# Eight raw weight tiles and three row tiles in the v half of a PEER layer

## The chip, the core and the metric

The kernel runs on one core of one Trainium2 chip. The metric is the device time of one execution in microseconds; the kernel before takes 3439.81 us, the median of three runs (3434.23 to 3440.13).

## What is computed

One layer of a diffusion backbone over 512 latent tokens of width 2048. The part that matters here is the second half of the layer, a retrieval of single-neuron experts (PEER). For every token 128 of 16384 experts are chosen (8 heads, 16 each), and the output is a weighted sum of their rows:

```python
u = u_tab[expert]
v = v_tab[expert]
act = jax.nn.gelu(jnp.einsum('nd,ned->ne', hb, u), approximate=False) * gate
return jnp.einsum('ne,ned->nd', act, v)
```

`u_tab` and `v_tab` have 16384 rows of 2048 float32 values, 128 MB each. The result, times a gain, is added to the residual stream and is the output.

## The kernel before

Float32 products are made of three passes in a rounded float32 format: each operand is split into `hi` (rounded) and `lo` (the remainder), and `mm3` (L102) issues hi x hi, hi x lo and lo x hi. For weights the split is made on the fly by `weights` (L93): a DMA on SyncE's queue brings a raw tile of 128x1024 float32 (512 KB, `raw_tile`, L88), ScalarE makes `whi` from it (L98), VectorE makes `wlo` (L99). There are four buffers for each of `raw`, `whi` and `wlo`. A raw buffer is free for the next DMA when its `wlo` is made; a `whi` or `wlo` buffer when the matmuls that read it are done.

The layer first computes modulations, projections, attention and convolution, the output projection and the choice of experts. Then come two halves over the expert tables:

- **The u half** (`u_block`, L515, 128 blocks). For 352 of the tokens the products with all 16384 experts are computed densely from streamed tiles of `uT`. The other 160 tokens go another way: `gather` (L715) lets GpSimd fetch one expert row for each of 128 token lanes (`row`, 128x2048, 1 MB, an indirect DMA, L723), 160 times in all, and `use_u` (L736) has VectorE form the dot products. The normalised activations lie in `HH` and `HL`, and in token-major form in `h2row` and `h2ext`.
- **The v half** (loop L846 to L882). The dense part is 16 groups of 8 units. A unit takes two tiles of `vb`, and accumulates two of the 16 output columns `m` in PSUM with 2 x 24 matmuls of 128x352. Every fourth column stays in PSUM over all groups (`held`, `hps` in the trace); the others are added by VectorE into `acc` (L877) after each unit. `Ah` and `Al` of a group are made a group ahead by `prepare` (L775): `load_group` (L767) loads `gt` and `gl` on SyncE's queue, VectorE multiplies (L784), ScalarE and VectorE split (L787, L789). Beside it, `gather` fetches 160 rows of `v`, and `use_v` (L743) has VectorE add each row, times its coefficient in `dots`, into the accumulator `accg` (L745). `gather` keeps two rows in flight: it fetches the next row after each use. `paced` spreads the 160 uses over the first 15 groups. In the last group `finish` (L829) adds everything to the residual and stores it.

Each engine runs its instructions in one fixed order, set when the program is built: a scheduler takes the program's order, gives tiles to buffers, and may move an instruction ahead of others that have to wait for a buffer. On VectorE the row accumulations, the `wlo` tiles, the `acc` additions and the `gl`/`Al` work thus stand in one queue; on SyncE the raw tiles and the `gt`/`gl` loads; on GpSimd the gathers. Memory is given out by pools: `vl` (L823), the v half's own pool, is opened after the u half's pools `us` and `hs` are closed and takes their room, so a tile in it waits until the last reader of what lay there is done. For `HH` and `HL` this is TensorE's last matmul of the u half. The pool `wp` lives through the whole kernel.

Of the kernel before, what the change touches and what calls it, by code (L numbers as in the profile page):

```python
# [10 lines left out]
F32 = mybir.dt.float32  # L11
# [3 lines left out]
AF = mybir.ActivationFunctionType  # L15
ALU = mybir.AluOpType
# [4 lines left out]
P = 128  # L21
T, D, L, KD = 512, 2048, 256, 16
# [5 lines left out]
ND = T - NG  # L28
# [14 lines left out]
def build(nc, tc, ap, es):  # L43
# [3 lines left out]
    wp = es.enter_context(pool("wp"))  # L47
# [38 lines left out]
    RAWB, HB, LB = 4, 4, 4  # L86

    def raw_tile(src, shape):  # L88
        raw = wp.tile(shape, F32, tag="raw", bufs=RAWB, name="raw")
        nc.sync.dma_start(raw, src)  # L90
        return raw

    def weights(src, eng=None):  # L93
        shape = list(src.shape)
        raw = raw_tile(src, shape)
        hi = wp.tile(shape, F32R, tag="whi", bufs=HB, name="whi")
        lo = wp.tile(shape, F32R, tag="wlo", bufs=LB, name="wlo")
        weights.hi = nc.scalar.activation(hi, raw, AF.Copy)  # L98
        weights.lo = (eng or nc.vector).tensor_tensor(lo, raw, hi.bitcast(F32), op=ALU.subtract)  # L99
        return hi, lo  # L100
# [28 lines left out]
    rings = {}  # L129

    def psum(role, name, *shape):
        banks = BANKS[role]
        turn = rings[role] = rings.get(role, -1) + 1
        t = pp.tile([P, 512], F32, tag=f"b{banks[turn % len(banks)]}", name=name)
        if len(shape) == 3:
            return t[:shape[0], 0:shape[1] * shape[2]].rearrange("p (a b) -> p a b", b=shape[2])
        return t[:shape[0], 0:shape[1]]
# [37 lines left out]
    def project(m, ctx):  # L175
        if m not in started:
            project_half(m, ctx, 0)
        project_half(m, ctx, 1)
        return started[m]
# [122 lines left out]
    def run_tasks(gen, n):  # L302
        for _ in range(n):
            if next(gen, 0) == 0:
                return
# [3 lines left out]
    with pool("att", side="right", **reuse) as att:  # L309
# [55 lines left out]
        for hd in range(NH):  # L365
            qps, _ = project(3 * hd, False)
# [23 lines left out]
    with pool("cnv", side="right", **reuse) as cnv:  # L390
# [11 lines left out]
        for g in range(8):  # L402
            cps, _ = project(24 + 3 * g, False)
# [5 lines left out]
            ups, _ = project(25 + 3 * g, False)  # L409
# [11 lines left out]
            bps, _ = project(26 + 3 * g, False)  # L421
# [59 lines left out]
    NS = P + NX  # L481
    h2row = gp.tile([P, KD, P], F32, name="h2row")
    h2ext = gp.tile([P, KD, P], F32, name="h2ext")
    exi = gp.tile([P, NS], I32, name="exi")
    gtg = gp.tile([P, NS], F32, name="gtg")
    dots = gp.tile([P, NS], F32, name="dots")
# [26 lines left out]
    mark = {}  # L513

    def u_block():  # L515
        i = u_block.n
        u_block.n += 1
        ps = psum("u", "sps", P, ND)
        for hf in range(2):
            w = weights(ap["uT"][i, hf])  # L520
            for k in range(8):
                kk = 8 * hf + k
                mm = mm3(ps, (w[0][:, k, :], w[1][:, k, :]), (HH[:, kk, 0:ND], HL[:, kk, 0:ND]), kk == 0, kk == KD - 1)
        mark["pe"], mark["dve"], mark["act"] = mm, weights.lo, weights.hi
        if i % 2 == 0:
            u_block.out = uo.tile([P, 2, ND], F32, tag="ug", bufs=2, name="ug")
        nc.scalar.activation(u_block.out[:, i % 2, :], ps, AF.Gelu)
        if i % 2 == 1:
            nc.scalar.dma_start(gu[i // 2], u_block.out)
# [124 lines left out]
    urow = us.enter_context(pool("urow", **reuse))  # L654
# [57 lines left out]
        if o + 4 == CH:  # L712
            nc.scalar.dma_start(gd[tok // CH], scatter.stg)

    def gather(tab, rp, use):  # L715
        rows = []

        def fetch():
            s = len(rows)
            if s == NS:  # L720
                return
            row = rp.tile([P, KD, P], F32, tag="row", bufs=2, name="row")
            nc.gpsimd.indirect_dma_start(out=row.rearrange("p k d -> p (k d)"), out_offset=None, in_=ap[tab],  # L723
                                         in_offset=bass.IndirectOffsetOnAxis(ap=exi[:, s:s + 1], axis=0))
            rows.append(row)

        fetch()
        fetch()
        yield
        for s in range(NS):  # L730
            with tc.issue_after(mark["dve"].ins):
                use(s, rows[s])
            fetch()
            yield
# [7 lines left out]

    def use_v(s, row):  # L743
        ag = accg[0 if s < P else 1]
        nc.vector.scalar_tensor_tensor(ag, row, dots[:, s:s + 1], ag, op0=ALU.mult, op1=ALU.add)  # L745

    def paced(gen, steps, units):
        state = [0, 0]

        def step():  # L750
            state[0] += 1
            want = min(steps, -(-state[0] * steps // units))
            while state[1] < want:
                state[1] += 1
                run_tasks(gen, 1)

        return step
# [4 lines left out]
    gat_u = None  # L762
# [31 lines left out]
    while u_block.n < 128:  # L794
        u_block()
        n = u_block.n
        if gat_u is None:
            gat_u = paced(gather("u", urow, use_u), NS + 1, 128 - n)
        gat_u()
        for x in built:  # L800
            scatter(*x)
        built = ready
        ready = []
        if hots:
            for _ in range(1):
                x = next(hots, 0)
                if x == 0:
                    hots = None
                    break
                if x:  # L810
                    ready.append(x)
        elif not built and va is None:
            gbs.close()
            pqs.close()
            va = vs.enter_context(pool("va", side="right", **reuse))
        if va and n >= 116:
            first = first or prepare(0, va)
            run_tasks(first, 1)
# [2 lines left out]
    hs.close()  # L821

    vl = vs.enter_context(pool("vl", **reuse))  # L823
    acc = vl.tile([P, KD, ND], F32, name="acc")
    accg = [vl.tile([P, KD, P], F32, name=f"accg{i}") for i in range(2)]
    for x in accg:
        nc.gpsimd.memset(x, 0.0)

    def finish(m):  # L829
        if m % 2 == 0:  # L830
            finish.x = vl.tile([P, 2, T], F32, tag="fin", bufs=2, name="xm")
            nc.sync.dma_start(finish.x, x1d[m:m + 2].rearrange("m p t -> p m t"))
        xm = finish.x[:, m % 2, :]
        g2c = mod2[:, 48 + m:49 + m]
        src = held[m] if m in held else acc[:, m, :]
        nc.vector.scalar_tensor_tensor(xm[:, 0:ND], src, g2c, xm[:, 0:ND], op0=ALU.mult, op1=ALU.add)
        tp = psum("fin", "tp", P, NG)
        nc.tensor.matmul(tp[:, 0:NX], accg[1][:, m, :], selq, start=True, stop=True)
        nc.tensor.transpose(tp[:, NX:NG], accg[0][:, m, :], ident)
        nc.vector.scalar_tensor_tensor(xm[:, ND:T], tp, g2c, xm[:, ND:T], op0=ALU.mult, op1=ALU.add)  # L840
        nc.sync.dma_start(ap["out"][:, m, :], xm)

    NGV = NGRP // 2
    held = {}
    gat_v = paced(gather("v", vl, use_v), NS + 1, 8 * (NGV - 1))
    for g in range(NGV):  # L846
        hi, lo = A[g]
        nxt = None
        if g + 1 < NGV:
            nxt = prepare(g + 1, va if g % 2 else vl)  # L850
        for dq in range(8):
            ws = [weights(ap["vb"][2 * g + q, dq]) for q in range(2)]
            mark["dve"] = weights.lo
            pss = []
            for x in range(2):
                m = 2 * dq + x
                if m % 4 == 3:
                    if g == 0:
                        held[m] = psum("held", "hps", P, ND)
                    pss.append(held[m])  # L860
                else:
                    pss.append(psum("v", "ops", P, ND))
            for q in range(2):
                w = ws[q]
                for x in range(2):
                    for b in range(NB):
                        mm3(pss[x], (w[0][:, b, P * x:P * x + P], w[1][:, b, P * x:P * x + P]),
                            (hi[:, NB * q + b, :], lo[:, NB * q + b, :]), q + b == 0 and (g == 0 or 2 * dq + x not in held),
                            q == 1 and b == NB - 1 and (g == NGV - 1 or 2 * dq + x not in held))
            for x in range(2):  # L870
                m = 2 * dq + x
                if m in held:
                    pass
                elif g == 0:
                    nc.scalar.activation(acc[:, m, :], pss[x], AF.Copy)
                else:
                    mark["dve"] = nc.vector.tensor_tensor(acc[:, m, :], acc[:, m, :], pss[x], op=ALU.add)  # L877
                if g == NGV - 1:
                    finish(m)
            gat_v()  # L880
            if nxt:
                run_tasks(nxt, 1)  # L882
# [69 lines left out]
```

## Time and profile before

| what | value |
|---|---|
| median of three runs | 3439.81 us |
| the profiled execution | 3443.56 us |
| its span, first to last instruction | 3441.8 us |
| TensorE busy (PE) | 3287.1 us, 96% of the span |
| VectorE busy (DVE) | 2492.6 us, 72% |
| ScalarE busy (ACT) | 1177.3 us, 34% |
| GpSimd busy (POOL) | 670.8 us, 19% |
| mean granted TensorE clock | 0.982 of full speed |
| HBM traffic | 909 MB, 264 GB/s over the span |

PE is TensorE, DVE VectorE, ACT ScalarE, POOL GpSimd and SP SyncE; a q behind a name is an engine's issuing part. The tiles carry the program's names. The durations of neighbouring matmuls overlap, so the pace of TensorE is read from how many run in a stretch, not from the duration of one. "DMA share" is the mean busy share of the core's 16 DMA engines.

### The profile page before, as it was taken

The page shows a single profiled execution, that of the slowest core. Times are in us where ns is not written, and L with a number is a line of the kernel's source. Part 1 is how long each engine was busy: PE and PEld are TensorE (multiplying, and loading weights), DVE is VectorE, ACT ScalarE, POOL GpSimd, SP SyncE. Part 2 cuts the span into 40 slices and gives each one's busy share as a digit, 9 for nine tenths or more (in the row PEclk, how much of TensorE's full clock was granted, in tenths as well). Part 3 has the DMA queues.
Part 4 walks back from the last instruction along what each step waited for, and adds up shares of the span by engine and source line. Part 5 has one row for each costly group of instructions (what it writes and reads, how often), then busy time and mean ns, then how long its engine had stood idle before and what let it go on. Part 6 is the DMA issues. An engine that isn't in the chain of part 4 may idle for free.

```text
span 3441.8 us, 48157 instructions
## 1 busy us (share of the span) xinstructions
PE 3287.1 (96%) x18951; PEld 3019.0 (88%) x18951; DVE 2492.6 (72%) x3648; ACT 1177.3 (34%) x1582; POOL 670.8 (19%) x402
## 2 busy tenths in 40 slices
PE   5899999999999988999999999999989989989999
PEld 1488888878887878999999999999989989989999
DVE  4444444888756888787888887676787887878885
ACT  3344444222324454333333333333222222322222
POOL 0000000000001663222211222222323223322320
PEclk9999999999999999999999999999999999999999
DMA  8722222888772226999999999998898998989986
GB/s 303 234 67 63 66 66 61 289 278 286 242 237 85 86 83 229 334 341 336 339 343 337 328 339 340 355 360 303 319 344 316 343 343 322 353 328 336 338 323 210
DMA packets 265316, 912.52 MB, mean 265 GB/s; under 512 B 23809, under 2 KB 77313, under 8 KB 222721
## 3 DMA queue, kind: packets, MB, share of 16 engines
q1 hardware_dynamic: 208208, 527.74, 44.6%
q0 software_dynamic: 46080, 335.56, 25.7%
q10 hardware_dynamic: 10800, 46.14, 3.4%
q8 instruction: 149, 2.44, 0.3%
q14 instruction: 79, 0.64, 0.1%
HBM read 854.82 MB, written 54.53 MB: 264 GB/s over the span
## 4 chain that ended last, share of the span: by engine, by line
PE 63%; DMA 19%; DVE 10%; issue 4%; POOL 2%; ACT 1%; SPq 0%; DVEq 0%; ACTq 0%; POOLq 0%
DMA row<-v,exi 11%; PE sps L105 8%; PE sps L103 8%; PE sps L104 8%; PE xps L103 4%; PE xps L105 4%; PE xps L104 4%; DVE accg L745 3%; DMA raw<-wada 3%; DVE wlo L99 3%; PE ops L105 3%; PE ops L103 2%; PE ops L104 2%; DMA row<-u,exi 2%; PE gps L709 2%
## 5 line engine op out<-in xcount | busy, mean ns | idle before, releaser
L98 ACT ACTIVATE whi<-raw 128x1024 fp32r<-128x1024 f32 x672 | 709.2, 1058 | 1642.6 <-PE sps L104 442.1
L99 DVE TENSOR_TENSOR wlo<-raw,whi 128x1024 fp32r<-128x1024 f32 x664 | 810.2, 1237 | 283.4 <-ACT whi L98 253.6
L105 PE MATMUL sps<-HH,wlo 128*128 128x352 f32 x2048 | 665.4, 325 | 21.4 <-DVE wlo L99 21.4
L103 PE MATMUL sps<-HH,whi 128*128 128x352 f32 x2048 | 671.8, 328 | 1.1 <-ACT whi L98 1.1
L104 PE MATMUL sps<-HL,whi 128*128 128x352 f32 x2048 | 663.7, 324 | 0.0
L105 PE MATMUL ops<-Ah,wlo 128*128 128x352 f32 x1536 | 505.4, 330 | 54.1 <-DVE wlo L99 54.0
L103 PE MATMUL ops<-Ah,whi 128*128 128x352 f32 x1536 | 503.2, 328 | 5.6 <-DVE acc L877 5.6
L104 PE MATMUL ops<-Al,whi 128*128 128x352 f32 x1536 | 499.5, 325 | 0.0
L745 DVE SCALAR_TENSOR_TENSOR accg<-row,dots,accg 128x2048 f32<-128x2048 f32 x160 | 375.6, 2348 | 160.1 <-DMA row<-v,exi 160.1
L723 POOL DMA_INDIRECT row<-v,exi x160 | 300.5, 1878 | 697.0 <-DVE accg L745 672.6
L105 PEld LDWEIGHTS sps<-HH,wlo 128*128 128x128 f32 x2048 | 387.9, 189 | 24.3 <-DVE wlo L99 24.3
L103 PEld LDWEIGHTS sps<-HH,whi 128*128 128x128 f32 x2048 | 388.3, 190 | 1.4 <-ACT whi L98 1.4
L104 PEld LDWEIGHTS sps<-HL,whi 128*128 128x128 f32 x2048 | 388.3, 190 | 0.0
L723 POOL DMA_INDIRECT row<-u,exi x160 | 226.1, 1413 | 785.1 <-DVE row L737 690.8
L105 PEld LDWEIGHTS ops<-Ah,wlo 128*128 128x128 f32 x1536 | 295.5, 192 | 61.1 <-DVE wlo L99 61.1
L737 DVE SCALAR_TENSOR_TENSOR row<-row,h2row 128x2048 f32<-128x2048 f32 x128 | 291.5, 2287 | 64.9 <-DMA row<-u,exi 64.7
L103 PE MATMUL xps<-HH,whi 128*128 128x512 f32 x768 | 306.0, 398 | 2.0 <-ACT whi L98 2.0
L105 PE MATMUL xps<-HH,wlo 128*128 128x512 f32 x768 | 303.6, 395 | 0.5 <-DVE wlo L99 0.5
L104 PE MATMUL xps<-HL,whi 128*128 128x512 f32 x768 | 303.2, 395 | 0.0
L103 PEld LDWEIGHTS ops<-Ah,whi 128*128 128x128 f32 x1536 | 293.9, 191 | 6.9 <-issue 4.1
L104 PEld LDWEIGHTS ops<-Al,whi 128*128 128x128 f32 x1536 | 294.7, 192 | 0.0
L99 POOL TENSOR_TENSOR wlo<-raw,whi 128x1024 fp32r<-128x1024 f32 x8 | 20.0, 2496 | 1003.4 <-ACT whi L98 1003.4
(274 smaller groups left out, 4943.0 us busy)
## 6 DMA issues: line engine op xcount, KB each, us to landing
raw<-uT SPq DMA_DIRECT2D x256, 512.0 KB
raw<-vb SPq DMA_DIRECT2D x256, 512.0 KB
raw<-wada SPq DMA_DIRECT2D x192, 512.0 KB
raw<-win SPq DMA_DIRECT2D x96, 512.0 KB
gu<-ug ACTq DMA_DIRECT2D x64, 352.0 KB
gd<-stg ACTq DMA_DIRECT2D x11, 2048.0 KB
gt<-gd SPq DMA_DIRECT2D x32, 704.0 KB
gl<-gu SPq DMA_DIRECT2D x32, 704.0 KB
```

Source lines behind the costliest of these rows:

```text
L98: weights.hi = nc.scalar.activation(hi, raw, AF.Copy)
L99: weights.lo = (eng or nc.vector).tensor_tensor(lo, raw, hi.bitcast(F32), op=ALU.subtract)
L103: nc.tensor.matmul(ps, lw[0], rw[0], start=start, stop=False)
L104: nc.tensor.matmul(ps, lw[0], rw[1], start=False, stop=False)
L105: return nc.tensor.matmul(ps, lw[1], rw[0], start=False, stop=stop)
L709: nc.tensor.matmul(gps[:, j, :], oj[:, j, :], oi[:, j, :], start=True, stop=True)
L723: nc.gpsimd.indirect_dma_start(out=row.rearrange("p k d -> p (k d)"), out_offset=None, in_=ap[tab], in_offset=bass.IndirectOffsetOnAxis(ap ...
L737: nc.vector.scalar_tensor_tensor(row, row, 1.0, h2row if s < P else h2ext, op0=ALU.mult, op1=ALU.mult, accum_out=dots[:, s:s + 1])
L745: nc.vector.scalar_tensor_tensor(ag, row, dots[:, s:s + 1], ag, op0=ALU.mult, op1=ALU.add)
```

## The change

Three things change, all for the v half. `raw_tile` deals its tiles out in turn over a list of pools, which is only `wp` until the v half begins; then `vl` is added, so that v tiles alternate between four buffers in `wp` and four in `vl`. The gather of `v` keeps three rows in flight instead of two. Room for both comes from the accumulators: `acc` has 12 columns instead of 16 (the four `held` ones were never written there), and the two accumulators of gathered rows are no tiles of their own: `h2row` and `h2ext`, dead after the u half, take their place. The first row of each is multiplied into it instead of added, so that the two memsets go.

```diff
     def raw_tile(src, shape):
-        raw = wp.tile(shape, F32, tag="raw", bufs=RAWB, name="raw")
+        raw_tile.n += 1
+        rings = raw_tile.rings
+        raw = rings[raw_tile.n % len(rings)].tile(shape, F32, tag="raw", bufs=RAWB, name="raw")
         nc.sync.dma_start(raw, src)
         return raw
+
+    raw_tile.n, raw_tile.rings = 0, [wp]
...
-    def gather(tab, rp, use):
+    def gather(tab, rp, use, ahead):
...
-            row = rp.tile([P, KD, P], F32, tag="row", bufs=2, name="row")
+            row = rp.tile([P, KD, P], F32, tag="row", bufs=ahead, name="row")
...
-        fetch()
-        fetch()
+        for _ in range(ahead):
+            fetch()
...
     def use_v(s, row):
         ag = accg[0 if s < P else 1]
+        if s in (0, P):
+            nc.vector.tensor_scalar(ag, row, dots[:, s:s + 1], None, op0=ALU.mult)
+            return
         nc.vector.scalar_tensor_tensor(ag, row, dots[:, s:s + 1], ag, op0=ALU.mult, op1=ALU.add)
...
-            gat_u = paced(gather("u", urow, use_u), NS + 1, 128 - n)
+            gat_u = paced(gather("u", urow, use_u, 2), NS + 1, 128 - n)
...
     vl = vs.enter_context(pool("vl", **reuse))
-    acc = vl.tile([P, KD, ND], F32, name="acc")
-    accg = [vl.tile([P, KD, P], F32, name=f"accg{i}") for i in range(2)]
-    for x in accg:
-        nc.gpsimd.memset(x, 0.0)
+    raw_tile.rings.append(vl)
+    acc = vl.tile([P, 12, ND], F32, name="acc")
+    accg = [h2row, h2ext]
...
-        src = held[m] if m in held else acc[:, m, :]
+        src = held[m] if m in held else acc[:, m - m // 4, :]
...
-    gat_v = paced(gather("v", vl, use_v), NS + 1, 8 * (NGV - 1))
+    gat_v = paced(gather("v", vl, use_v, 3), NS + 1, 8 * (NGV - 1))
...
-                    nc.scalar.activation(acc[:, m, :], pss[x], AF.Copy)
+                    nc.scalar.activation(acc[:, m - m // 4, :], pss[x], AF.Copy)
...
-                    mark["dve"] = nc.vector.tensor_tensor(acc[:, m, :], acc[:, m, :], pss[x], op=ALU.add)
+                    mark["dve"] = nc.vector.tensor_tensor(acc[:, m - m // 4, :], acc[:, m - m // 4, :], pss[x], op=ALU.add)
```

The change moves instructions on three engines. On SyncE, the queue of the loads, from the first v tile on; before:

```order
L90 DMA raw<-vb 128x1024 x8
L769 DMA gt<-gd 128x11x128
L832 DMA xm<-x1d 128x2x512
L90 DMA raw<-vb 128x1024
L832 DMA xm<-x1d 128x2x512
L90 DMA raw<-vb 128x1024
L772 DMA gl<-gu 128x2x704
L90 DMA raw<-vb 128x1024 x4
L769 DMA gt<-gd 128x11x128
```

and now:

```order
L92 DMA raw<-vb 128x1024 x12
L838 DMA xm<-x1d 128x2x512
L776 DMA gt<-gd 128x11x128
L92 DMA raw<-vb 128x1024 x2
L838 DMA xm<-x1d 128x2x512
L779 DMA gl<-gu 128x2x704
L92 DMA raw<-vb 128x1024 x4
L776 DMA gt<-gd 128x11x128
```

The first `gt` has 12 raw tiles ahead of it instead of 8, the second 18 instead of 14, and so on to the end. With the semaphores shown, the fourth to eighth v tile in SyncE's order now read as follows (DVE, PE: the engine whose progress is waited for; DMAHW: an earlier DMA):

```order
L92 DMA raw<-vb 128x1024 [waits DMAHW5_49,DVE_49]
L92 DMA raw<-vb 128x1024 [waits DMAHW4_49,PE_49]
L92 DMA raw<-vb 128x1024
L92 DMA raw<-vb 128x1024 [waits DMAHW6_49]
L92 DMA raw<-vb 128x1024 [waits DMAHW7_49]
```

The four behind the first row are the tiles of the new ring; the first of them is the first v tile of the program, and waits for TensorE. The other four, of the old ring, stand ahead of it. On ScalarE, at the end of the u half (`ug`: the last results of the u half; `whi<-raw`: the conversion of weight tiles), before:

```order
L529 DMA gu<-ug 128x704
L98 ACTIVATE whi<-raw 128x1024 x2
L527 ACTIVATE ug<-sps 128x352
L98 ACTIVATE whi<-raw 128x1024 x2
L527 ACTIVATE ug<-sps 128x352
L529 DMA gu<-ug 128x704
L98 ACTIVATE whi<-raw 128x1024
L787 ACTIVATE Ah<-gl 128x1408
```

and now:

```order
L533 DMA gu<-ug 128x704
L531 ACTIVATE ug<-sps 128x352 x2
L533 DMA gu<-ug 128x704
L102 ACTIVATE whi<-raw 128x1024 x5
L881 ACTIVATE acc<-ops 128x352
```

The four conversions of v tiles that stood between the last two results of the u half stand behind both. On VectorE at the same place (`dots`: the last coefficients; `row,dots`: the use of a gathered row), before:

```order
L741 TENSOR_TENSOR dots<-dots,gtg 128x4
L99 TENSOR_TENSOR wlo<-raw,whi 128x1024 x5
L784 TENSOR_TENSOR gl<-gl,gt 128x11x4x32
L99 TENSOR_TENSOR wlo<-raw,whi 128x1024 x2
L789 TENSOR_TENSOR Al<-gl,Ah 128x1408
L99 TENSOR_TENSOR wlo<-raw,whi 128x1024
L745 SCALAR_TENSOR_TENSOR accg_19691<-row,dots,accg_19691 128x2048 x2
```

and now:

```order
L745 TENSOR_TENSOR dots<-dots,gtg 128x4
L103 TENSOR_TENSOR wlo<-raw,whi 128x1024 x3
L750 TENSOR_SCALAR h2row<-row,dots 128x2048
L103 TENSOR_TENSOR wlo<-raw,whi 128x1024 x2
L752 SCALAR_TENSOR_TENSOR h2row<-row,dots,h2row 128x2048
L791 TENSOR_TENSOR gl<-gl,gt 128x11x4x32
L103 TENSOR_TENSOR wlo<-raw,whi 128x1024 x2
```

The first use of a row stands behind the second v tile's `wlo` (the first tile of the three is the u half's last) instead of the seventh's.

## Rows read from the trace of the kernel before

**Rows 1.** The head of the page.

```profile
span 3441.8 us, 48157 instructions
```

**Rows 2.** Busy time by stretch; (x) counts instructions.

```profile
core 0: us, PE busy (x) PEld busy (x) DVE busy (x) ACT busy (x) POOL busy (x), PEclk, DMA share, GB/s
2300.00:2364.00 64.00, 61.73 (x375) 61.44 (x374) 39.94 (x37) 20.46 (x27) 11.11 (x8) 0.97 0.84 309
2364.00:3376.00 1012.00, 952.29 (x5787) 944.07 (x5786) 811.12 (x630) 298.00 (x285) 303.26 (x162) 0.97 0.90 333
3376.00:3441.00 65.00, 61.53 (x402) 61.10 (x401) 34.25 (x56) 11.67 (x11) 0.00 (x0) 1.00 0.56 183
```

**Rows 3.** The same view, in six stretches of 30 us.

```profile
2360.00:2390.00 30.00, 30.00 (x189) 30.00 (x188) 16.18 (x12) 11.33 (x16) 10.18 (x6) 1.00 0.88 326
2450.00:2480.00 30.00, 30.00 (x189) 30.00 (x188) 21.94 (x18) 8.13 (x8) 9.36 (x4) 1.00 0.84 303
2540.00:2570.00 30.00, 22.94 (x130) 22.44 (x130) 23.28 (x17) 8.70 (x8) 6.35 (x4) 0.89 0.92 333
2960.00:2990.00 30.00, 29.92 (x187) 29.63 (x186) 25.29 (x21) 7.44 (x7) 8.34 (x6) 1.00 0.95 366
2990.00:3020.00 30.00, 29.73 (x183) 29.16 (x182) 24.40 (x19) 11.88 (x11) 10.38 (x5) 1.00 0.98 358
3230.00:3260.00 30.00, 30.00 (x189) 30.00 (x189) 24.68 (x20) 7.46 (x8) 10.25 (x6) 1.00 0.96 368
```

**Rows 4.** Waits in 2364 to 3376: us in total, times, longest.

```profile
ACT whi L98 <- DMA raw<-vb: 243.5, 66, 15.2
...
DVE accg L745 <- DMA row<-v,exi: 160.1, 80, 5.9
...
PE ops L105 <- DVE wlo L99: 54.0, 22, 6.1
```

**Rows 5.** VectorE in order of time at a stall: start, us, what [idle before].

```profile
2627.54 2.35 DVE L745 SCALAR_TENSOR_TENSOR accg<-row,dots,accg 128x2048 f32<-128x2048 f32 x1 [5.95 <-DMA row<-v,exi]
2629.80 1.22 DVE L99 TENSOR_TENSOR wlo<-raw,whi 128x1024 fp32r<-128x1024 f32 x1
```

**Rows 6.** TensorE at the same stall.

```profile
2631.08 0.43 PE L105 MATMUL ops<-Ah,wlo 128*128 128x352 f32 x1 [3.53 <-DVE wlo L99]
```

**Rows 7.** SyncE's queue at the same stall.

```profile
2621.62 0.38 SPq L772 DMA_DIRECT2D gl<-gu  x1
2631.05 6.86 SPq L90 DMA_DIRECT2D raw<-vb  x4
```

**Rows 8.** Busy time by stretch, columns as in Rows 2, of this stall.

```profile
2627.50:2631.10 3.60, 0.07 (x2) 0.02 (x1) 3.56 (x3) 0.67 (x1) 0.94 (x1) 1.00 0.42 171
2631.10:2635.20 4.10, 4.10 (x16) 4.10 (x17) 4.10 (x4) 0.00 (x0) 0.73 (x1) 0.58 0.77 274
```

**Rows 9.** DMA queues in 2364 to 3376: packets, MB, share of 16 engines.

```profile
q1 hardware_dynamic: 82680, 167.56, 47.2%
q0 software_dynamic: 23040, 167.78, 42.1%
```

**Rows 10.** The chain that ended last: start, us, what; three gathers.

```profile
2366.95 6.66 DMA row<-v,exi
...
2379.42 10.47 DMA row<-v,exi
...
2613.82 13.62 DMA row<-v,exi
```

**Rows 11.** GpSimd in order of time at the handover.

```profile
2363.23 3.55 POOL L827 MEMSET accg<- 128x2048 f32 x2 [27.19 <-PE sps L105]
2366.95 0.94 POOL L723 DMA_INDIRECT row<-v,exi  x1 [0.16 <-issue]
```

**Rows 12.** SyncE's queue at the handover, v tiles issued before it.

```profile
2341.53 20.32 SPq L90 DMA_DIRECT2D raw<-vb  x7
```

**Rows 13.** SyncE's queue, one v tile issued alone.

```profile
2357.66 0.33 SPq L90 DMA_DIRECT2D raw<-vb  x1
```

**Rows 14.** GB/s moved in 2357 to 2363, in 40 slices of 0.15 us.

```profile
GB/s 82 109 0 0 0 0 0 27 0 0 55 109 328 82 109 246 246 246 437 437 410 382 191 191 55 0 0 0 0 0 0 0 0 0 0 0 218 137 27 191
```

**Rows 15.** The page's groups of the two conversions: busy us, mean ns.

```profile
L98 ACT ACTIVATE whi<-raw 128x1024 fp32r<-128x1024 f32 x672 | 709.2, 1058 | 1642.6 <-PE sps L104 442.1
L99 DVE TENSOR_TENSOR wlo<-raw,whi 128x1024 fp32r<-128x1024 f32 x664 | 810.2, 1237 | 283.4 <-ACT whi L98 253.6
```

## The prediction

> **What bounds the kernel now.** I began with the page's head for the span [rows 1], then cut the span where the work changes [rows 2]. Everything the edit touches is issued from 2364 us on. In the stretch 2364 to 3376 the v half runs with its row gathers; the last 65 us have none. In the middle stretch TensorE is busy 952.3 of 1012 us, so it stands still for 59.7 us, and its granted clock is 0.97 on average, so some of its busy time is slow. A full window shows the pace: 189 matmuls in 30 us at clock 1.00 [rows 3], 158.7 ns each. The 5787 matmuls of the stretch need 5787 x 0.1587 = 918 us. So 94 us of 1012 are lost: 60 standing still and 34 at the lower clock (1.2 instead of 2.4 GHz).
>
> The waits say why it stands still [rows 4]: TensorE waits 54.0 us for `wlo`, VectorE's rounding remainder of a weight tile; VectorE waits 160.1 us for gathered rows; ScalarE waits 243.5 us for raw weight tiles. One stall shows how they hang together. VectorE reaches a row's accumulation and stands 5.95 us for the row [rows 5]; the `wlo` queued behind it ends at 2631.0, and TensorE has waited 3.53 us for it [rows 6]. SyncE issues no raw tile from 2621.6 to 2631.05 [rows 7], since a raw buffer comes free only when its `wlo` is made. So the 16 DMA engines fall to a share of 0.42 while TensorE is idle, and the 4.1 us after it run at clock 0.58 [rows 8]. A late row costs TensorE its idle time, then about as long at a lower clock, and costs the DMA engines time that they need later.
>
> The second limit lies close. Over the stretch the DMA engines have a busy share of 0.90 and move 333 GB/s [rows 2]; the queues' packets sum to 47.2 + 42.1 + 0.4 = 89.7% [rows 9], which is 908 us of work in 1012. VectorE is busy 811 us [rows 2]: 88% of 918, not the bound.
>
> **The change part by part.**
>
> *Third row tile.* 160 rows in 1012 us is one per 6.3 us. With two tiles a row is asked for two uses ahead, 12.6 us; the row of the example took 13.62 us to land [rows 10]. With three it has 18.9 us. The 160.1 us of VectorE's row waits (longest 5.9) should mostly go.
>
> *Four more raw tiles.* The raw tile in use was asked for four conversions ahead, 4 x 3.8 = 15 us at TensorE's pace of 24 matmuls a tile; now it is eight, 30 us. A VectorE pause of 6 to 10 us no longer empties SyncE's queue. The order shows that the extra tiles really run ahead: every `gt` load now stands four raw tiles later.
>
> *Smaller accumulator, dead activations as accumulators.* Four of 16 columns stay in PSUM already and were never written, so nothing is computed differently. The POOL memsets, 3.55 us ahead of the first gather [rows 11], go, so the first row is asked for at 2363.3 instead of 2366.95. Two of 160 accumulations become plain products; taken as 2.35 us as now, at nothing, since VectorE has spare time.
>
> *The handover from the u half: a new cost.* Before, seven v tiles are asked for by 2361.85 [rows 12] and TensorE crosses at 2363.2 without a gap: 30.00 of 30 us busy [rows 3]. Now tiles alternate between the old ring and the new one, and the first v tile falls to the new ring, whose room is the u half's activations. It waits for the last u matmul, and ScalarE's conversion of it (and of the second, which has long landed) stands behind. Its price: a tile asked for alone at 2357.66 [rows 13] is moved by about 2360.75 (the 0.15 us slices fall silent there [rows 14]), 3.1 us; then 1.06 us `whi` and 1.24 us `wlo` [rows 15]; 5.4 us of idle TensorE. What the clock costs after such a gap: in 2540 to 2570 130 matmuls ran, 20.6 us worth, with 7.06 us idle [rows 3], so 2.3 us. Together 8 us. Lower bound: 3 us, if the wlo and the clock are hidden. Upper: the third tile's `wlo` now stands behind the first row on VectorE, and rows took 6.66 us (quiet) to 10.47 us there [rows 10]; with three rows and four tiles asked for at once I allow 5 us more, 13 in all.
>
> *The sum.* TensorE's side: 918 + 8 = 926 us. The DMA side: 908 us, plus tiles drawn into the stretch: three no longer prefetched before it and four more ahead at its end, 7 x 0.524 MB = 3.7 MB at 333/0.90 = 370 GB/s, 10 us, so 918 us at a share of 1. The engines hold 0.95 and 0.96 over whole 30 us windows, at 366 and 368 GB/s [rows 3]; that is the nearest row for a queue that no longer runs dry, and I take 0.955: 918/0.955 = 961 us. The larger side decides: 961 instead of 1012, a saving of 51 us. The 64 us ahead and the last 65 us stay. The profiled execution took 3443.6 us (span 3441.8 and 1.8 around it); 3443.6 - 51 = 3392.6. It lies 3.8 us above the median of the runs, so on the median's scale I forecast 3389 us.
>
> The Trainium skill, "DMA: Bandwidth & Descriptors" (Specifications), puts HBM at about 358 GB/s per core; the stretch's 340.3 MB would then need 951 us, an estimate that would close off anything better than 3379. The windows above 358 [rows 3] and the 437 GB/s slices of a tile moved alone [rows 14] speak against it as a limit here, and the skill's "Perfetto Trace Analysis" (Roofline) says that a core running alone may draw more than that share.
>
> **The rivals.**
>
> *TensorE-bound.* The stalls go and DMA keeps up at a share of 918/926 = 0.99: 1012 - 926 = 86 us saved, 3354 us. For it: whole windows of 30.00 us busy at share 0.96. Against: of the 30 us windows I cut, one has 0.98, at 358 GB/s, and TensorE still idle 0.3 us in it [rows 3]; the other good ones have 0.95 or 0.96.
>
> *The queues stay coupled.* VectorE still takes rows and tiles in one fixed order, so a late row still holds up `wlo`, and more transfers at once only make each slower. Share 0.92 to 0.93, as the window with the large stall has it (0.92): 998 to 987 us, 14 to 25 us saved, 3415 to 3426.
>
> *No effect.* If SyncE stood at `gt` loads so that extra raw tiles were never filled, and rows were bandwidth-bound anyway, nothing would move but the handover's few us: about 3440. The order speaks against it.
>
> *Slower: the handover is all that changes.* Its place is the first v tile behind the last u matmul; its price 8 to 13 us. It decides if the steady part saves less than that, which needs the DMA share to stay under 918/1004 = 0.915, since the late rows would then be a bandwidth limit and not a buffer limit: 3448 to 3453 us. The gap is nearly sure to appear; that nothing pays for it is not, because in the example the DMA engines were at 0.42 while a row was late.
>
> **How the numbers follow.** Forecast 0.52, TensorE-bound 0.17, coupled 0.18, no effect 0.06, slower 0.07. Predicted 3389 us. The range takes in the coupled case to its end (3426, and some us for the handover's upper price) and reaches to the TensorE-bound one: 3356 to 3430; that leaves out the last two and a little of the second, under 0.2. A difference of 0.2%, 7 us, is about what a measurement of this kernel can tell from none. Faster 0.87, same 0.06, slower 0.07.
>
> **What would show it.** Right: a TensorE gap of 5 to 6 us at about 2363; VectorE's waits for rows under 60 us; ScalarE's waits for raw tiles under 100; a DMA share near 0.95 from the handover to the end of the gathers, that stretch 50 us shorter; TensorE's idle time in it about 25 us, with fewer slow windows. Wrong: the share at 0.90 with the row waits still there (coupled, or slower), or a stretch under 940 us (TensorE-bound). If the row waits fall and TensorE waits as long for `wlo`, VectorE's order is the limit.

## The result, and the profile after

| | before | after |
|---|---|---|
| median (lowest to highest) | 3437.02 us (3432.45 to 3440.13), 4 runs | 3359.46 us (3353.41 to 3364.3), 4 runs |
| ratio, 95% interval | | 0.9768 (0.9748 to 0.9787) |
| profiled execution | 3443.56 us | 3353.41 us |

The kernel is about 78 us faster. The time lies inside the predicted range, but near its lower end and 30 us below the forecast of 3389: the case that came true is the rival called TensorE-bound (3354 us).

The two profiled executions lie 90 us apart, and not all of that is the change. The u half ended at 2363.2 us before and ends at 2355.7 now, though nothing in it was edited; so 7.5 us lie ahead of the v half. From there to the end of the span it was 3441.8 - 2363.2 = 1078.6 us and is 3351.2 - 2355.7 = 995.5: the v half is **83 us** shorter. The rival had 86.

The page of the kernel after, its head and the engines' totals:

```profile
span 3351.2 us, 48181 instructions
...
PE 3252.6 (97%) x18951; PEld 2994.8 (89%) x18951; DVE 2488.7 (74%) x3648; ACT 1179.5 (35%) x1582; POOL 689.5 (21%) x400
```

The same cuts as [rows 2], moved to where the work changes now: the handover, the stretch with gathers, the tail.

```profile
core 0: us, PE busy (x) PEld busy (x) DVE busy (x) ACT busy (x) POOL busy (x), PEclk, DMA share, GB/s
2355.00:2364.00 9.00, 3.80 (x15) 3.34 (x14) 2.36 (x2) 4.00 (x5) 2.82 (x3) 0.78 0.80 286
2364.00:3290.00 926.00, 926.00 (x5813) 925.63 (x5811) 812.79 (x636) 300.81 (x285) 322.96 (x157) 1.00 0.95 366
3290.00:3350.00 60.00, 57.15 (x374) 56.73 (x372) 30.73 (x51) 10.60 (x10) 0.00 (x0) 1.00 0.43 149
```

The middle line is the main result: 926.00 us of TensorE in 926.00 us, where [rows 2] has 952.3 of 1012 at clock 0.97. TensorE does not stand still once in this stretch, and its clock averages 1.00. The DMA share is 0.95 as forecast, yet the time saved is 83 us and not 51. (The cut at 2364 lies behind the handover gap here, and the one at 3290 some 4 us behind the point that 3376 marks before; on the same work the 1012 us have become 1012 - 83 = 929.)

TensorE in order of time at the handover: start, us, what [idle before]. ScalarE follows in the second fence.

```profile
2360.92 0.66 PE L107 MATMUL ops<-Ah,whi 128*128 128x352 f32 x1 [5.20 <-ACT whi L102]
```

```profile
2359.81 2.00 ACT L102 ACTIVATE whi<-raw 128x1024 fp32r<-128x1024 f32 x2 [3.59 <-DMA raw<-vb]
```

The one gap at the handover is 5.20 us, because ScalarE waits for the first v tile, which waits for the u half's room. The price of the clock behind it, and then the steady pace:

```profile
2360.92:2367.70 6.78, 6.78 (x25) 6.61 (x26) 4.63 (x4) 2.96 (x4) 0.73 (x1) 0.56 1.02 427
2367.70:2380.00 12.30, 12.30 (x80) 12.30 (x79) 12.01 (x9) 6.66 (x8) 5.07 (x3) 1.00 1.03 420
```

For 6.8 us the granted clock is 0.56, the lower of the two levels (1.2 GHz) for nearly all of it; what TensorE did before was to stand for 5.20 us. 25 matmuls ran in these 6.78 us; at the pace of the second line they take 3.84, so the clock costs about 2.9 us. Then it is 2.4 GHz, up to the tail.

The waits in 2364 to 3290 (us in total, times, longest) that answer to [rows 4]:

```profile
ACT whi L102 <- DMA raw<-vb: 16.5, 6, 2.8
DVE h2row L750 <- DMA row<-v,exi: 2.1, 1, 2.1
DVE h2row L752 <- DMA row<-v,exi: 0.3, 1, 0.3
```

VectorE's wait for rows fell from 160.1 to 2.4 us, ScalarE's for raw tiles from 243.5 to 16.5, and TensorE's for `wlo` is gone.

The DMA queues in the same stretch (packets, MB, share of 16 engines), against [rows 9]:

```profile
q1 hardware_dynamic: 83518, 170.63, 50.3%
q0 software_dynamic: 22935, 166.92, 44.4%
```

Nearly the same bytes, and less time for them. Before, q1 moved 167.56 MB in 0.472 x 1012 = 478 us, 351 GB/s at a full share; now 170.63 MB in 0.503 x 926 = 466 us, 366 GB/s. q0 went from 394 to 406 GB/s in the same way. Both with the 0.3% of q8: 0.950 x 926 = 880 us of packet time, where the forecast had 918. (The unit is the busy time of all 16 engines together.)

### The profile page after: what moved, and what is told of

Same layout as the page of the kernel before. It is cut to its first block, busy times and chain, and to the rows that moved or that the text cites. A ratio compares the mean times of both kernels' runs of the same rounds, so it can differ in the third digit from the quotient of the medians.

```text
span 3351.2 us, 48181 instructions
## 1 busy us (share of the span) xinstructions
PE 3252.6 (97%) x18951; PEld 2994.8 (89%) x18951; DVE 2488.7 (74%) x3648; ACT 1179.5 (35%) x1582; POOL 689.5 (21%) x400
## 3 DMA queue, kind: packets, MB, share of 16 engines
q1 hardware_dynamic: 208208, 527.74, 45.4%
## 4 chain that ended last, share of the span: by engine, by line
PE 81%; DMA 9%; DVE 5%; POOL 2%; issue 2%; ACT 1%; SPq 0%; DVEq 0%; ACTq 0%; POOLq 0%
PE sps L107 8%; PE sps L109 8%; PE sps L108 8%; PE ops L107 7%; PE ops L109 7%; PE ops L108 7%; PE xps L107 4%; PE xps L108 4%; PE xps L109 4%; DMA raw<-wada 4%; DMA row<-u,exi 3%; PE hps L107 2%; PE hps L109 2%; PE hps L108 2%; PE gps L713 2%
## 5 line engine op out<-in xcount | busy, mean ns | idle before, releaser
L109 PE MATMUL ops<-Ah,wlo 128*128 128x352 f32 x1536 | 492.9, 322 | 0.0
L727 POOL DMA_INDIRECT row<-v,exi x160 | 325.8, 2036 | 614.0 <-DVE h2row L752 440.8
L752 DVE SCALAR_TENSOR_TENSOR h2row<-row,dots,h2row 128x2048 f32<-128x2048 f32 x127 | 298.0, 2346 | 0.4 <-DMA row<-v,exi 0.3
```

Source lines behind the costliest of these rows:

```text
L109: return nc.tensor.matmul(ps, lw[1], rw[0], start=False, stop=stop)
```

## The experiments

The change has two halves that the prediction did not separate: a third row tile, and four more raw tiles with their handover. **Theory R**: the rows were late, and the third row tile alone brings the gain. **Theory T**: the raw tiles bring it, since a pause of VectorE no longer empties SyncE's queue. Edits are against the changed kernel where nothing else is said. Each ratio is to the kernel before, run beside it on the same chip, where its median was 3444.6 to 3446.7 us.

### The two halves apart

Only the third row tile (`e1_row3`); the raw tiles stay four, and with them goes the handover:

```diff
     vl = vs.enter_context(pool("vl", **reuse))
-    raw_tile.rings.append(vl)
```

> Only the third row tile, with the smaller accumulator; four raw tiles as before. If late rows are what stalls (theory R), VectorE's wait for rows falls from 160 us to under 20 and nearly all of the gain stays; since the first v tiles are prefetched as before, the handover gap of 5.2 us and its slow 6.8 us are not there either: 3350 to 3360 us. If the raw tiles carry the gain (theory T), rows land in time but raw tiles are still late whenever VectorE pauses: 3400 to 3425 us.

Measured: 3353.82 us (3349.09 to 3362.22), ratio 0.9743 (0.9722 to 0.9763): the whole gain.

Only the raw tiles (`e2_raw8`):

```diff
-    gat_v = paced(gather("v", vl, use_v, 3), NS + 1, 8 * (NGV - 1))
+    gat_v = paced(gather("v", vl, use_v, 2), NS + 1, 8 * (NGV - 1))
```

> Only the four more raw tiles; two rows in flight as before. Theory R: VectorE still waits some 150 us for rows and TensorE stalls behind wlo, little gained and the handover paid: 3410 to 3445 us. Theory T: the late rows remain, but conversions run up to four tiles ahead of TensorE, so that a pause of 6 us is covered: 3360 to 3375 us with row waits still over 100 us.

Measured: 3438.48 us (3432.38 to 3447.24), ratio 0.9992 (0.9979 to 1.0006): nothing.

Both edits together (`e0_room_only`): two row tiles, four raw tiles, and only the smaller accumulator and the rows' sums in the dead activations are left of the change.

> Only the room: accumulator of 12 columns, h2row and h2ext as accumulators, no memsets; two rows and four raw tiles. Both theories: same as before within 7 us, about 3440 us, with VectorE waiting about 150 us for rows as before. If the layout itself or the memsets mattered, it would be over 10 us faster.

Measured: 3446.31 us (3437.32 to 3452.38), ratio 0.9994 (0.998 to 1.0009): nothing.

The waits in 2375 to 3265 of these kernels, 890 us inside the stretch with gathers in each. First the kernel before:

```profile
ACT whi L98 <- DMA raw<-vb: 214.9, 60, 14.0
DVE accg L745 <- DMA row<-v,exi: 150.7, 74, 5.9
...
PE ops L105 <- DVE wlo L99: 48.2, 20, 6.1
```

Eight raw tiles, two row tiles:

```profile
DVE h2row L752 <- DMA row<-v,exi: 132.8, 60, 6.5
...
PE ops L109 <- DVE wlo L103: 45.4, 23, 6.5
ACT whi L102 <- DMA raw<-vb: 16.5, 6, 2.8
DVE h2ext L752 <- DMA row<-v,exi: 15.4, 11, 4.2
```

Four raw tiles, three row tiles:

```profile
ACT whi L102 <- DMA raw<-vb: 158.1, 47, 7.6
...
DVE h2row L752 <- DMA row<-v,exi: 3.2, 1, 3.2
...
PE ops L109 <- DVE wlo L103: 2.2, 2, 1.9
```

This decides between R and T. With eight raw tiles ScalarE's wait for them falls from 214.9 to 16.5 us, and TensorE waits for `wlo` as before (45.4 against 48.2), because VectorE still stands for rows (132.8 + 15.4 = 148 us against 150.7). With the third row tile ScalarE goes on waiting for raw tiles, 158.1 us, and it costs TensorE almost nothing. The largest wait in the table was a wait with slack behind it; the smaller one, on VectorE, was the one that ended last.

### The handover

Run beside it: the changed kernel once more (`after_again`), and a version in which the tiles go four and four to the two rings instead of by turns, so that the first four v tiles need no room of the u half (`e3_handover`):

```diff
-        raw = rings[raw_tile.n % len(rings)].tile(shape, F32, tag="raw", bufs=RAWB, name="raw")
+        raw = rings[(raw_tile.n - raw_tile.n0) // RAWB % len(rings)].tile(shape, F32, tag="raw", bufs=RAWB, name="raw")
...
     raw_tile.rings.append(vl)
+    raw_tile.n0 = raw_tile.n + 1
```

> The changed kernel once more, on the same chip as the three others, as the base for them: 3353 to 3364 us, one gap of about 5 us at the handover and none after it.

> The changed kernel, but v tiles are dealt four to the old ring, four to the new, so that the first four do not wait for the last u matmul. If the handover is the gap of 5.2 us and 6.8 us at half clock, it costs 8.6 us, and this is 8 to 9 us faster than the changed kernel, about 3351 us, with TensorE busy without a gap at the handover. If the gap only moves (the first rows or the fifth tile come late instead), within 3 us of the changed kernel.

Measured: 3353.48 us (3352.01 to 3362.25), ratio 0.9741 (0.9722 to 0.9761), for the changed kernel; 3359.49 us (3356.88 to 3361.15), ratio 0.9753 (0.9735 to 0.977), for the other deal. The expected gain of 8 to 9 us did not come. The gap at the handover is gone, and another stands 22 us later. SyncE's queue of this version, then ScalarE, then TensorE:

```profile
2362.94 0.33 SPq L92 DMA_DIRECT2D raw<-vb  x1
2364.47 0.38 SPq L776 DMA_DIRECT2D gt<-gd  x1
2364.94 10.51 SPq L92 DMA_DIRECT2D raw<-vb  x4
```

```profile
2381.68 1.06 ACT L102 ACTIVATE whi<-raw 128x1024 fp32r<-128x1024 f32 x1 [12.84 <-DMA raw<-vb]
```

```profile
2382.79 0.66 PE L107 MATMUL ops<-Ah,whi 128*128 128x352 f32 x1 [6.83 <-ACT whi L102]
```

The first tile of the new ring, now the fifth, is issued behind a `gt` load of 704 KB and beside three rows; it lands after 2381, and TensorE stands 6.83 us, with 5.8 us behind it at a mean granted clock of 0.51, the lower level. So the wait was moved, not removed. That also settles what the raw tiles are worth in the change: the version without them crosses the handover without a gap and has three small gaps between 2396 and 2410, 3.4 us together, with the clock at 1.00; the change has none of these and pays 5.2 + 2.9 us at the handover. The two cannot be told apart by their times.

### Why two row tiles were too few

A fourth row tile (`e7_row4`: the version with the third row tile alone, and `use_v, 4`):

> Four row tiles in flight, four raw tiles (third-row kernel with a fourth). Theory B (the third row covers the round trip of a row, and nothing is left to cover): within 5 us of the third row alone, 3350 to 3358 us. Theory L (rows are short of bandwidth, and each further row in flight takes a larger share): some 10 us or more off, in either direction, since raw tiles then come late.

Measured: 3358.22 us (3356.38 to 3359.6), ratio 0.9743 (0.9717 to 0.9768), the same as three. The DMA issues of the gathers (op, count, median us from issue to landing) in 2375 to 3265, with two row tiles (`e0_room_only`) and with three (`e1_row3`):

```profile
row<-v,exi POOLq DMA_INDIRECT x140, 9.0
```

```profile
row<-v,exi POOLq DMA_INDIRECT x155, 9.4
```

With four it is 9.1. The landing hardly changes with the number of rows in flight. So a row tile's round is about 9.0 us of landing, 2.35 us of use on VectorE and some 0.3 us until the next issue, 11.6 us (an estimate from these rows). With two tiles that is about one row per 5.8 us; TensorE at full pace consumes one per 926/160 = 5.79 us. There was no reserve at all: whatever VectorE did between two uses came on top, and the measured pace was 1012/160 = 6.3 us. Three tiles allow 3.9 us.

How much of the loss is the round itself and how much VectorE's fixed order, in which a row's use waits behind `wlo` and additions? The next kernel (`e10_no_acc`, against `e0_room_only`) takes 168 additions of about 0.52 us from VectorE and leaves the rows at two tiles; the partial sums of the token groups 1 to 14 are left out of its output:

```diff
-                    mark["dve"] = nc.vector.tensor_tensor(acc[:, m - m // 4, :], acc[:, m - m // 4, :], pss[x], op=ALU.add)
+                    if g == NGV - 1:
+                        mark["dve"] = nc.vector.tensor_tensor(acc[:, m - m // 4, :], acc[:, m - m // 4, :], pss[x], op=ALU.add)
```

> The room-only kernel (two rows, four raw tiles) without VectorE's additions into the accumulator in groups 1 to 14: those partial sums are left out of the output. It takes about 84 us of work off VectorE and changes no transfer. Theory V (late rows hurt because VectorE's work and its row waits together fill its time): with 84 us free the waits for rows stay near 150 us or grow, but TensorE's waits for wlo fall below 20 us: 3360 to 3385 us. Theory P (the round trip of a row with two in flight sets the pace by itself): 3430 to 3450 us.

Measured: 3416.21 us (3406.27 to 3422.42), ratio 0.9923 (0.9897 to 0.9949): 29 us by the medians, about a third of the third row tile's gain for 87 us less work on VectorE. It lies between the two expected ranges and in neither. Its waits in 2375 to 3265:

```profile
ACT whi L102 <- DMA raw<-vb: 305.0, 90, 8.8
DVE h2row L752 <- DMA row<-v,exi: 164.9, 81, 5.7
...
PE ops L109 <- DVE wlo L103: 38.8, 26, 3.1
...
DVE h2ext L752 <- DMA row<-v,exi: 26.5, 10, 4.8
```

The time that VectorE got back went mostly into longer waits for rows (191 us against 136.0 + 13.6 in the kernel with the additions): the rows came every 6.06 us (127 uses from 2372.0 to 3135.5) instead of every 6.39. That is about half of the way from 6.39 to TensorE's 5.79; the profiled execution, 3406.27 us, is the fastest of its four. So VectorE's own work makes a third to a half of the loss, and the round the rest. With VectorE mostly waiting for rows the round was 2 x 6.06 = 12.1 us and not the 11.6 estimated from the median landing. The exact split stays open: the additions also mark where the rows' uses are placed, so this kernel's order is not the old one minus the additions.

### What the DMA engines could carry

The forecast took 0.955 as the best share. To see the ceiling, loads that nothing reads were added to the changed kernel, one per unit of the first 15 groups of the v half: 256 KB (`e5a_pad256`), then 512 KB (`e5b_pad512`) on SyncE:

```diff
+            if g < NGV - 1:
+                pad = vl.tile([P, 512], F32, tag="pad", bufs=2, name="pad")
+                nc.sync.dma_start(pad, ap["vb"][2 * g, dq].rearrange("p b n -> p (b n)")[:, 0:512])
```

> The changed kernel with one more load of 256 KB, that nobody reads, in each of the 120 units with gathers: 31.5 MB more, 9%. Theory C (the DMA engines have a ceiling near the share of 0.955 that the prediction took, 366 GB/s): 371 MB take 1014 us instead of 926, so about 3440 us. Theory N (no ceiling there; deeper queues move more): under 15 us slower than the changed kernel, 3355 to 3372 us, at 400 GB/s.

> The same with 512 KB: 63 MB more, 18%. Theory C: 403 MB at 366 GB/s take 1100 us, about 3530 us. Theory N with a ceiling at the best 30 us window of the changed kernel, 408 GB/s: 988 us, about 3418 us.

Measured: 3460.08 us (ratio 1.0038, 1.0023 to 1.0053) and 3486.13 us (1.0116, 1.0087 to 1.0146). Inconclusive as they stand: the pads were not spread over the v half but bunched in its first 400 (256 KB) to 590 us (512 KB), where SyncE's queue stands for a free pad and the raw tiles behind it come late. So a third version gives the 512 KB to ScalarE's queue, each issued behind a conversion, evenly spread (`e5c_even512`):

```diff
+            if g < NGV - 1:
+                pad = vl.tile([P, 1024], F32, tag="pad", bufs=2, name="pad")
+                with tc.issue_after(weights.hi.ins):
+                    nc.scalar.dma_start(pad, ap["vb"][2 * g, dq].rearrange("p b n -> p (b n)"))
```

> The changed kernel with one more load of 512 KB in each of the 120 units with gathers, now issued by ScalarE behind a conversion of that unit, so that the scheduler cannot pull the loads together: 403 MB in the stretch. At TensorE's pace of 926 us this needs 436 GB/s. With the forecast's ceiling of 366 GB/s it takes 1100 us, about 3530 us. With a ceiling of 390 to 400, as in the bunched run at share 1.00, 1009 to 1034 us, about 3440 to 3460 us. Without one, 3355 to 3365 us.

Measured: 3433.81 us (3426.06 to 3435.72), ratio 0.9956 (0.994 to 0.9972). The same 890 us by the view of [rows 2], of this kernel and then of the changed one:

```profile
2375.00:3265.00 890.00, 847.77 (x5178) 841.01 (x5177) 721.23 (x564) 259.49 (x253) 287.11 (x143) 0.98 1.03 403
```

```profile
2375.00:3265.00 890.00, 890.00 (x5592) 889.63 (x5591) 782.09 (x611) 288.57 (x272) 317.13 (x154) 1.00 0.96 368
```

The engines carry 403 GB/s for 890 us, at a share that the view reads as 1.03. The changed kernel at TensorE's full pace needs 368. So the DMA engines could carry at least 9% more than the changed kernel asks of them; by the forecast they should have held it 4% below TensorE's pace (961 us against 926).

### A version beyond both

In the u half of the kernel VectorE also waits for rows, with two tiles; its waits in 1400 to 2355, with the u half untouched (`e1_again`, the third row tile alone on the same chip):

```profile
DVE row L741 <- DMA row<-u,exi: 107.9, 54, 5.0
...
PE sps L109 <- DVE wlo L103: 6.7, 7, 2.2
```

The next kernel (`e9_urow3`) gives the u half a third row tile too, in room taken from two small tiles:

```diff
-            tt = gb.tile([P, 3, P], F32, tag="ijt", bufs=2, name="ijt")
+            tt = gb.tile([P, 3, P], F32, tag="ijt", bufs=1, name="ijt")
...
-                oi = gb.tile([P, 4, P], F32, tag="oi", bufs=4, name="oi")
+                oi = gb.tile([P, 4, P], F32, tag="oi", bufs=2, name="oi")
...
-            gat_u = paced(gather("u", urow, use_u, 2), NS + 1, 128 - n)
+            gat_u = paced(gather("u", urow, use_u, 3), NS + 1, 128 - n)
...
-    raw_tile.rings.append(vl)
```

> The third row alone once more, on the same chip, as the base for the u half's third row: 3350 to 3360 us.

> The third-row kernel with a third row tile in the u half too (room from two one-hot tiles and one transposed tile less). VectorE waits 111 us for rows in the u half, but TensorE waits only 21 us for wlo there. Theory V: VectorE has room in the u half, so at most the 10 us of gaps around 2229 to 2327 and their slow clock go: 0 to 12 us faster than the third row alone. If row waits cost by their length, 50 us or more.

Measured: 3355.73 us (3349.11 to 3360.14), ratio 0.9737 (0.9714 to 0.976), without it; 3347.28 us (3344.3 to 3349.96), ratio 0.9715 (0.9694 to 0.9735), with it. This is the lowest median of all; it is below the kernel before and the changed one, though its interval overlaps that of the version without, so the step of 8 us by the medians is likely and not proved. The end of the u half, in the two:

```profile
2200.00:2350.00 150.00, 144.00 (x889) 142.26 (x888) 106.83 (x100) 48.79 (x65) 36.79 (x24) 1.00 0.91 343
```

```profile
2200.00:2350.00 150.00, 150.00 (x933) 150.00 (x933) 106.22 (x99) 51.66 (x67) 35.65 (x22) 1.00 0.90 342
```

6 us of TensorE gaps are gone. VectorE waited 108 us for rows of u in these 955 us, and 150.7 for rows of v in 890 in the kernel before; the first cost a small fraction of the second. A likely reason is VectorE's spare time: it was busy or waiting for rows in 740.5 + 107.9 = 848 of 955 us, 89%, in the u half, and in 710.9 + 150.7 = 862 of 890, 97%, in the v half. No run changes this share alone, so the reason is argued and not shown.

## Why the prediction was right and wrong

*What bounds the kernel now.* The chain in the stall that the prediction read [rows 5, 6] was the cause: a late row, the `wlo` behind it, TensorE. Shown by the third row tile alone, which removes all three. The other half of that reading, SyncE's raw tiles that stop with it [rows 7], was an effect without a price: `e2_raw8` took ScalarE's waits for raw tiles away and gained nothing.

*Third row tile.* Right in kind: the row waits went, 160.1 to 2.4 us where under 60 was asked for. The prediction had the count that matters in hand, 6.3 us a row and tiles two ahead, but held it against a single landing of 13.62 us [rows 10] instead of a tile's whole round, which shows that two tiles left no reserve.

*Four more raw tiles.* Wrong. The order was read rightly, the tiles do run ahead, and ScalarE's waits fell from 243.5 to 16.5 us. But the time that this returns is none, with two row tiles (`e2_raw8` against `e0_room_only`) and with three (`after_again` against `e1_row3`).

*The handover.* Right: 5.20 us of gap for a forecast of 5.4, 2.9 us by the clock for 2.3; 8.1 in place of 8. The gathers start behind the last u matmul and no longer behind the memsets, as said. The allowance of 5 us for `wlo` behind the first rows was not needed.

*The sum.* This is the step that failed. The range held because it had been drawn down to the rival's time, not because the forecast's limit was the one that decided. TensorE's side, 918 + 8 = 926 us, is nearly what the same work took, 929 us. The DMA side, "908 us, plus ... 10 us" at a share of 0.955, 961 us, was taken as the larger and decided. Two things in it were wrong. First, the 908 us of packet time were treated as work that takes as long whenever it is done; in the changed kernel nearly the same bytes took 880 us. Second, 0.955 came from two good windows [rows 3], in a kernel whose DMA engines ran only as fast as the buffers let them; that is a share that was asked for, not one that they could not pass. That 0.95 was then measured is luck: TensorE's pace set the length of the stretch, and 880 us of packets happen to be 0.95 of it. The change ran its first 30 us at 408 GB/s, and `e5c_even512` held 403 for 890 us. In the window that the prediction set against the rival, 0.98 at 358 GB/s with TensorE still idle 0.3 us, VectorE waited 5.6 us for rows; it showed late rows and no ceiling. So the time that a late row costs the DMA engines was not time "that they need later".

These are three of the changed kernel's first four stretches of 30 us, columns as in [rows 2]; the first holds the end of the handover gap, and the one left out, 2420 to 2450, has 0.92 at 345 GB/s:

```profile
2360.00:2390.00 30.00, 29.08 (x166) 28.91 (x166) 26.00 (x18) 13.68 (x16) 10.32 (x5) 0.89 1.03 408
2390.00:2420.00 30.00, 30.00 (x191) 30.00 (x190) 22.85 (x15) 12.33 (x15) 9.59 (x5) 1.00 1.03 402
2450.00:2480.00 30.00, 30.00 (x191) 30.00 (x190) 27.35 (x23) 9.77 (x9) 10.73 (x5) 1.00 1.00 388
```

*The bandwidth of a page.* The estimate of 951 us by the Trainium skill's figure of about 358 GB/s per core ("DMA: Bandwidth & Descriptors", Specifications) fell: the whole stretch moved 366 GB/s. The Trainium skill's other statement, that a core running alone may draw more than its share and is bounded by its DMA engines at about 435 GB/s in all ("Perfetto Trace Analysis", Roofline), agrees with the 403 GB/s of `e5c_even512`; that run shows the first half of it, and no run here reaches the bound.

*The rivals.* TensorE-bound came true, 83 us saved for its 86; it had been given a chance of 0.17. Coupled: fell, the share rose and the waits went. No effect, and slower by the handover alone: fell for the change. No effect describes `e2_raw8`, which has the raw tiles and gets nothing (ratio 0.9992).

*What would show it.* The gap, the row waits, the raw waits and the share came as named. "TensorE's idle time in it about 25 us" (0 was measured) and "a stretch under 940 us" separated the forecast from its rival, and both went to the rival.

## What to carry to other kernels

A buffer count is judged by the tile's whole round (issue, landing, use) divided by the tiles in flight, held against the pace of the consumer. Here the two were equal, 5.8 us each, and one more tile was worth about 90 us. The largest wait in the table may be worth nothing, as ScalarE's for raw tiles was here; what a wait costs is seen from what stands behind it on its engine, and proved by a run that removes it alone.

A resource is not shown to be the bound by a high share while others wait for it. Here its packet time fell from 908 to 880 us and its share rose from 0.90 to 0.95 when the waits went, and an added load that nothing reads showed that it could carry more still.

New room that is still in use should not take the first of the tiles that come next. Moving that tile later is no gain by itself: here it then stood in a queue behind other loads, and the gap came 22 us later.

## What was not expected of the hardware

- A gather of a row tile lands in 9.0, 9.4 and 9.1 us with two, three and four of them in flight.
- The same bytes took less packet time when more was in flight: 351 to 366 GB/s per full share on q1, 394 to 406 on q0, and shares read up to 1.03. Why the packets took less time, no run here tells.
- TensorE's best pace is a little above the one taken from [rows 3]: 191 matmuls in 30 us instead of 189. Over the whole 926 us, which begin with 3.7 us at the lower clock, it was 5813, 159.3 ns each (some records may be missing), beside the 158.7 of the prediction.
- Four raw tiles behind a `gt` load and beside three gathers took 10.51 us to issue on SyncE, the first of them alone 8.86, where one issued by itself takes 0.33 [rows 13].
